# Cross-entropy over 32,000 classes: new row grouping, a third buffer, a tapered last group and transposed results

## The chip, the cores and the metric

The kernel runs on one core of one Trainium2 chip. The metric is the device time of one execution in microseconds (us).

## The reference

For each of 16 x 512 = 8192 rows of 32,000 float32 logits the loss is the log of the sum of exponentials minus the logit at the label. The kernels leave out the maximum, which this data (standard normal) allows.

```python
def reference(logits, labels):                  # (16, 512, 32000) f32, (16, 512) i32
    m = np.max(logits, axis=-1, keepdims=True)
    lse = np.log(np.sum(np.exp(logits - m), axis=-1)) + m.squeeze(-1)
    log_probs = logits - lse[..., np.newaxis]
    return -log_probs[np.arange(16)[:, None], np.arange(512), labels]
```

## The kernel before

The rows are cut into 64 groups of 128, one row per partition. Partition p holds rows 64p to 64p+63, so that one group takes rows 64 apart. SyncE (SP) issues the loads, ScalarE (ACT) takes the exponential in place and sums along the row, GpSimd (POOL) gathers the 8192 label logits with 64 indirect loads. HBM here names the memory of logits and results (`in_logits_dram` and `out_dram` in the profile); a transfer lands when the profile shows it complete. The first 61 groups are loaded in halves of 16,000 columns into two buffers, the last three in pieces of 4,000.

```python
lg_pg  = lg.rearrange("(p g) v -> p g v", g=G)              # group g: rows p*64 + g
out_pg = out.rearrange("b s -> (b s)").rearrange("(p g) -> p g", g=G)
data_pool = ctx.enter_context(tc.tile_pool(name="data", bufs=2))
fine_pool = ctx.enter_context(tc.tile_pool(name="fine", bufs=5))
nc.sync.dma_start(out=labs64[:], in_=labels_pg)             # before the logits
# ... indices, 64 gathers on GpSimd ...
for g in range(G):
    if g >= G - FINE_GROUPS:                                # 3 groups, WF = 4000
        # ... tf from fine_pool, 8 pieces a group, the same two calls ...
    else:
        for c in range(C):                                  # W = 16000, C = 2
            t = data_pool.tile([P, W], FP32)
            nc.sync.dma_start(out=t[:], in_=lg_pg[:, g, c * W:(c + 1) * W])
            nc.scalar.activation(out=t[:], in_=t[:], func=Exp, accum_out=stats_col(g, c))

def finalize(lo, hi):
    # ... totals = reduce_sum(stats), on VectorE ...
    # ... logsum = Ln(totals), on ScalarE ...
    # ... res = logsum - lab_logit, on VectorE ...
    nc.scalar.dma_start(out=out_pg[:, lo:hi], in_=res[:, lo:hi])
finalize(0, G - 1)
finalize(G - 1, G)        # 128 results, one per partition, 4 B each, 256 B apart in HBM
```

The softmax here doesn't subtract the row's maximum and nothing guards it: scores larger than these inputs give would overflow.

## Time and profile before

| | before |
|---|---|
| time, median of 3 | 2439.99 us |
| span of the profile | 2438.7 us |
| moved, mean rate | 1048.77 MB, 430 GB/s |
| start to start of two 16,000-column exponentials, steady part | 18.90 us |
| last load lands / last store issued / end | 2430.8 / 2436.21 / 2438.7 us |

The first lines are from the page of the kernel before. A row of digits shows the busy tenths of 40 slices of the span; GB/s is what the DMA engines moved in each.

```profile
span 2438.7 us, 851 instructions
...
ACT  4777766777677767777677767777677767777697
...
DMA  9999999999999999999999999999999999999998
GB/s 404 437 420 422 435 437 435 429 429 437 437 436 428 431 435 437 435 432 428 435 436 436 435 427 434 436 437 435 427 432 436 437 435 425 434 437 432 426 430 360
```

The DMA engines are full in every slice but the last (digit 9, 90% or more; a DMA share of 1.00 from 240 to 2380 us), ScalarE is not (72% of the span): the time to move 1048 MB is the time of the kernel. The chain of work that ended last, by line, on the same page:

```profile
DMA t<-in_logits_dram 61%; ACT t L85 34%; DMA tf<-in_logits_dram 2%; ACT tf L76 2%; ACT L101 0%; ACT L76 0%; ACTq L85 0%; ACT logsum L101 0%; SPq L84 0%; DVE res L105 0%; SPq L48 0%; ACTq L109 0%; ACTq L76 0%
```

The 34% of ScalarE does not mean that ScalarE limits anything. The chain goes from a load back to the exponential that freed its buffer. The costliest groups on that page tell it (busy us, mean ns of one | idle before it and what ended the idle time):

```profile
L85 ACT ACTIVATE t<-t 128x16000 f32<-128x16000 f32 x122 | 1651.4, 13536 | 642.9 <-DMA t<-in_logits_dram 642.9
...
L101 ACT ACT_TABLE_LOAD x2 | 2.6, 1283 | 0.0
```

Two exponentials of the steady part in the timeline, 18.90 us from start to start:

```profile
2297.67 13.54 ACT L85 ACTIVATE t<-t 128x16000 f32<-128x16000 f32 x1 [5.27 <-DMA t<-in_logits_dram]
...
2316.57 13.54 ACT L85 ACTIVATE t<-t 128x16000 f32<-128x16000 f32 x1 [5.27 <-DMA t<-in_logits_dram]
```

Each 13.5 us exponential waits 642.9 / 121 = 5.3 us for its load (the first of the 122 is booked apart).

A load lands 24.1 us after issue and the previous one lands 18.9 us before it, so 5.2 us of the 24.1 were spent in the queue: it never ran dry. The second line is the last store of all, 128 results of 4 B; it landed 1.4 us after issue. The timeline of the end (start us, us, engine, line):

```profile
2430.84 3.54 ACT L76 ACTIVATE tf<-tf 128x4000 f32<-128x4000 f32 x1 [1.11 <-DMA tf<-in_logits_dram]
...
2434.49 1.28 ACT L101 ACT_TABLE_LOAD   x1
...
2435.78 0.20 ACT L101 ACTIVATE logsum<-totals 128x1 f32<-128x1 f32 x1
2436.02 0.16 DVE L105 TENSOR_TENSOR res<-logsum,lab_logit 128x1 f32<-128x1 f32 x1 [1.35 <-ACT logsum L101]
2436.21 0.34 ACTq L109 DMA_DIRECT2D out_dram<-res  x1
```

The last exponential starts when the last load has landed. The store of the last group is issued at 2436.21 and the span ends at 2438.7, 2.5 us later.

### The profile page before, as it was taken

Reading aid. Unit: us, or ns where it says so; the run is one execution under the profiler, and the core shown is the slowest. Engines: PE = TensorE matmul, PEld = TensorE weight load, DVE = VectorE, ACT = ScalarE, POOL = GpSimd, SP = SyncE. Lnnn points to the kernel's source line nnn. Section 1 sums busy time; section 2 is a strip of 40 time slices with the busy share of each in tenths; the row PEclk is TensorE's granted clock in tenths of the full one; section 3 lists DMA queues with packets and bytes.
Section 4 is the critical chain, followed back from the end, with each engine's and each line's share of the span. In section 5 each row is a group of like instructions: output and inputs, shape, how many; then the busy total and the mean of one; then the engine's idle time right before and its main releaser. Section 6 shows DMA issues by size and latency. Waiting matters only on the chain.

```text
span 2438.7 us, 851 instructions
## 1 busy us (share of the span) xinstructions
DVE 1.7 (0%) x5; ACT 1754.4 (72%) x298; POOL 61.2 (3%) x70
## 2 busy tenths in 40 slices
DVE  0000000000000000000000000000000000000000
ACT  4777766777677767777677767777677767777697
POOL 3222000000000000000000000000000000000000
DMA  9999999999999999999999999999999999999998
GB/s 404 437 420 422 435 437 435 429 429 437 437 436 428 431 435 437 435 432 428 435 436 436 435 427 434 436 437 435 427 432 436 437 435 425 434 437 432 426 430 360
DMA packets 23510, 1048.77 MB, mean 430 GB/s; under 512 B 4688, under 2 KB 4816, under 8 KB 4816
## 3 DMA queue, kind: packets, MB, share of 16 engines
q1 hardware_dynamic: 21168, 1048.65, 99.6%
q0 software_dynamic: 2048, 0.04, 0.1%
q10 hardware_dynamic: 288, 0.03, 0.0%
q14 instruction: 6, 0.05, 0.0%
HBM read 1048.67 MB, written 0.03 MB: 430 GB/s over the span
## 4 chain that ended last, share of the span: by engine, by line
DMA 63%; ACT 36%; issue 0%; ACTq 0%; SPq 0%; DVE 0%
DMA t<-in_logits_dram 61%; ACT t L85 34%; DMA tf<-in_logits_dram 2%; ACT tf L76 2%; ACT L101 0%; ACT L76 0%; ACTq L85 0%; ACT logsum L101 0%; SPq L84 0%; DVE res L105 0%; SPq L48 0%; ACTq L109 0%; ACTq L76 0%
## 5 line engine op out<-in xcount | busy, mean ns | idle before, releaser
L85 ACT ACTIVATE t<-t 128x16000 f32<-128x16000 f32 x122 | 1651.4, 13536 | 642.9 <-DMA t<-in_logits_dram 642.9
L76 ACT ACTIVATE tf<-tf 128x4000 f32<-128x4000 f32 x24 | 84.7, 3530 | 14.6 <-DMA tf<-in_logits_dram 14.6
L57 POOL DMA_INDIRECT lab_logit<-in_logits_dram,idx x64 | 60.5, 945 | 186.8 <-DMA lab_logit<-in_logits_dram,idx 184.2
L85 ACT ACTIVATION_READ_ACCUMULATOR t<-t 128x1 f32 x122 | 22.7, 186 | 0.0
L85 ACT ACT_TABLE_LOAD x1 | 1.3, 1283 | 23.3 <-DMA t<-in_logits_dram 23.3
L76 ACT ACTIVATION_READ_ACCUMULATOR tf<-tf 128x1 f32 x24 | 4.5, 187 | 0.0
L101 ACT ACT_TABLE_LOAD x2 | 2.6, 1283 | 0.0
L96 DVE TENSOR_REDUCE totals<-stats 128x63 f32<-128x504 f32 x1 | 0.7, 678 | 2394.9 <-ACT tf L76 2394.9
L76 ACT ACT_TABLE_LOAD x1 | 1.3, 1283 | 0.8 <-DVE res L105 0.8
L66 DVE MEMSET stats<- 128x504 f32 x1 | 0.5, 478 | 0.9 <-PEq L127 0.9
L101 ACT ACTIVATE logsum<-totals 128x63 f32<-128x63 f32 (+1 forms) x2 | 0.5, 229 | 0.0
L105 DVE TENSOR_TENSOR res<-logsum,lab_logit 128x63 f32<-128x63 f32 (+1 forms) x2 | 0.4, 192 | 2.2 <-ACT logsum L101 2.2
L53 POOL TENSOR_TENSOR idx<-idx,labs 128x64 int32<-128x64 int32 x1 | 0.3, 318 | 1.8 <-DMA labs<-in_labels_dram 1.8
L96 DVE TENSOR_REDUCE totals<-stats_last 128x1 f32<-128x8 f32 x1 | 0.2, 161 | 36.4 <-ACT tf L76 36.4
L51 POOL IOTA idx<- 128x64 int32 x1 | 0.2, 172 | 0.4 <-PEq L138 0.4
L127 POOL MEMSET const-uint8-127<- 128x1 uint8 x1 | 0.1, 118 | 0.0
L127 POOL MEMSET const-bfloat16-1.0<- 128x1 bf16 x1 | 0.1, 113 | 0.0
L127 POOL MEMSET const-float32-0.0<- 128x1 f32 x1 | 0.1, 98 | 0.2 <-issue 0.2
L127 POOL MEMSET const-float32-1.0<- 128x1 f32 x1 | 0.1, 104 | 0.0
## 6 DMA issues: line engine op xcount, KB each, us to landing
t<-in_logits_dram SPq DMA_DIRECT2D x122, 8000.0 KB, 24.1
tf<-in_logits_dram SPq DMA_DIRECT2D x24, 2000.0 KB, 20.1
lab_logit<-in_logits_dram,idx POOLq DMA_INDIRECT x64, 33.4
labs<-in_labels_dram SPq DMA_DIRECT2D x1, 64.0 KB, 1.9
out_dram<-res ACTq DMA_DIRECT2D x1, 31.5 KB, 9.1
out_dram<-res ACTq DMA_DIRECT2D x1, 0.5 KB, 1.4
```

What stands on the lines that cost most here:

```text
L51: nc.gpsimd.iota(idx[:], pattern=[[V, G]], base=0, channel_multiplier=G * V)
L53: nc.gpsimd.tensor_tensor(out=idx[:], in0=idx[:], in1=labs32, op=mybir.AluOpType.add)
L57: nc.gpsimd.indirect_dma_start(out=lab_logit[:, g:g + 1], out_offset=None, in_=lg, in_offset=bass.IndirectOffsetOnAxis(ap=idx[:, g:g + 1], ...
L66: nc.vector.memset(stats[:], 0.0)
L76: nc.scalar.activation(out=tf[:], in_=tf[:], func=mybir.ActivationFunctionType.Exp, accum_out=stats_col(g, c),)
L85: nc.scalar.activation(out=t[:], in_=t[:], func=mybir.ActivationFunctionType.Exp, accum_out=stats_col(g, c),)
L96: nc.vector.reduce_sum(out=totals[:, lo:hi], in_=stats[:, lo:hi, :] if hi <= G - 1 else stats_last[:], axis=mybir.AxisListType.X,)
L101: nc.scalar.activation(out=logsum[:, lo:hi], in_=totals[:, lo:hi], func=mybir.ActivationFunctionType.Ln,)
L105: nc.vector.tensor_tensor(out=res[:, lo:hi], in0=logsum[:, lo:hi], in1=lab_logit[:, lo:hi], op=mybir.AluOpType.subtract,)
L127: nc = _bacc.Bacc("TRN2", target_bir_lowering=False, num_devices=1)
```

## The change

Its intent: hold more loads in flight (three buffers), end on pieces that shrink so that little work is left after the last load, load one table set that serves both exponential and log, and group neighbouring rows, which makes a group's results one contiguous run of the output. Labels and results then have to be transposed, on TensorE. The last group's 128 results are stored without a transpose. The core of the diff (cuts marked):

```diff
-    lg_pg = lg.rearrange("(p g) v -> p g v", g=G)
-    out_pg = out.rearrange("b s -> (b s)").rearrange("(p g) -> p g", g=G)
+    lg_gp = lg.rearrange("(g p) v -> g p v", p=P)
+    out_gp = out.rearrange("b s -> (b s)").rearrange("(g p) -> g p", p=P)
-    data_pool = ctx.enter_context(tc.tile_pool(name="data", bufs=2))
-    fine_pool = ctx.enter_context(tc.tile_pool(name="fine", bufs=5))
+    data = ctx.enter_context(tc.tile_pool(name="data", bufs=3))
+    TAPER = [11200, 8000, 5600, 3500, 2000, 1100, 600]
-    nc.sync.dma_start(out=labs64[:], in_=labels_pg)
+    nc.scalar.dma_start(out=labs64[:], in_=labels_gp)          # [64, 128]
+    nc.scalar.preload_act_table_set("natural_log_exp_and_others")
+    # ... labels to float, transposed on TensorE, back to int32 ...
-    # ... groups as above, the last 3 in pieces of 4000 ...
+    # ... 63 groups in halves of 16000 ...
+    spaces = [[0, 3, 5], [1, 2, 4], [6]]                       # pieces that share a buffer
+    for i, n in enumerate(TAPER):
+        nc.sync.dma_start(out=place[i], in_=lg_gp[G - 1, :, starts[i]:starts[i] + n])
+    for i, n in enumerate(TAPER):
+        nc.scalar.activation(out=place[i], in_=place[i], func=EXP, accum_out=sums_last[:, i:i + 1])
-    finalize(0, G - 1)
-    finalize(G - 1, G)
+    # ... totals, Ln, subtract for 63 groups ...
+    nc.tensor.transpose(res_t[:], res[:], ident[:])
+    nc.vector.tensor_copy(out=res_out[:], in_=res_t[:])
+    nc.scalar.dma_start(out=out_gp[0:G - 1, :], in_=res_out[:])
+    nc.vector.reduce_sum(out=part[:], in_=sums_last[:, 0:NT - 1], axis=mybir.AxisListType.X)
+    nc.scalar.activation(out=logsum_last[:], in_=sums_last[:, NT - 1:NT], func=LN, bias=part[:])
+    # ... subtract ...
+    nc.scalar.dma_start(out=out_gp[G - 1, :].unsqueeze(1), in_=res_last[:])
```

The scheduler puts the log and the store of the first 63 groups ahead of the seven tapered pieces in ScalarE's program.

More of the change, by code (lines that the diff above doesn't have):

```diff
@@ L7 @@
 from concourse._compat import with_exitstack
+from concourse.masks import make_identity
 FP32 = mybir.dt.float32
 I32 = mybir.dt.int32
+EXP = mybir.ActivationFunctionType.Exp
+LN = mybir.ActivationFunctionType.Ln
+ALU = mybir.AluOpType
 @with_exitstack
@@ L23 @@
     B, S, V = logits.shape
-    N = B * S
     P = 128
-    G = N // P
-    assert N % P == 0
+    G = B * S // P
     W = 16000
     C = V // W
-    assert V % W == 0
-    WF = 4000
-    CF = V // WF
-    FINE_GROUPS = 3
-    assert V % WF == 0
-    lg = logits.rearrange("b s v -> (b s) v")
-    lg_pg = lg.rearrange("(p g) v -> p g v", g=G)
-    labels_pg = labels.rearrange("b s -> (b s)").rearrange("(p g) -> p g", g=G)
-    out_pg = out.rearrange("b s -> (b s)").rearrange("(p g) -> p g", g=G)
@@ L43 @@
-    data_pool = ctx.enter_context(tc.tile_pool(name="data", bufs=2))
-    fine_pool = ctx.enter_context(tc.tile_pool(name="fine", bufs=5))
-    persist = ctx.enter_context(tc.tile_pool(name="persist", bufs=1))
-    labs64 = persist.tile([P, G], mybir.dt.int64)
-    nc.sync.dma_start(out=labs64[:], in_=labels_pg)
+    lg = logits.rearrange("b s v -> (b s) v")
+    lg_gp = lg.rearrange("(g p) v -> g p v", p=P)
+    labels_gp = labels.rearrange("b s -> (b s)").rearrange("(g p) -> g p", p=P)
+    out_gp = out.rearrange("b s -> (b s)").rearrange("(g p) -> g p", p=P)
@@ new lines @@
+    data = ctx.enter_context(tc.tile_pool(name="data", bufs=3))
+    persist = ctx.enter_context(tc.tile_pool(name="persist", bufs=1))
+    psum = ctx.enter_context(tc.tile_pool(name="psum", bufs=1, space=bass.MemoryType.PSUM))
+    TAPER = [11200, 8000, 5600, 3500, 2000, 1100, 600]
+    assert sum(TAPER) == V
+    NT = len(TAPER)
+    labs64 = persist.tile([G, P], mybir.dt.int64)
+    nc.scalar.dma_start(out=labs64[:], in_=labels_gp)
+    nc.scalar.preload_act_table_set("natural_log_exp_and_others")
@@ L50 @@
+    labs32 = labs64[:].bitcast(I32).rearrange("g (p two) -> g p two", two=2)[:, :, 0]
+    ident = persist.tile([P, P], FP32)
+    make_identity(nc, ident[:])
+    labs_f = persist.tile([G, P], FP32)
+    nc.vector.tensor_copy(out=labs_f[:], in_=labs32)
+    labs_t = psum.tile([P, G], FP32)
+    nc.tensor.transpose(labs_t[:], labs_f[:], ident[0:G, 0:G])
+    labs = persist.tile([P, G], I32)
+    nc.vector.tensor_copy(out=labs[:], in_=labs_t[:])
     idx = persist.tile([P, G], I32)
-    nc.gpsimd.iota(idx[:], pattern=[[V, G]], base=0, channel_multiplier=G * V)
@@ L52 @@
-    labs32 = labs64[:].bitcast(I32).rearrange("p (g two) -> p g two", two=2)[:, :, 0]
-    nc.gpsimd.tensor_tensor(out=idx[:], in0=idx[:], in1=labs32, op=mybir.AluOpType.add)
+    nc.gpsimd.iota(idx[:], pattern=[[P * (V >> 8), G]], base=0, channel_multiplier=V >> 8)
+    nc.vector.tensor_scalar(out=idx[:], in0=idx[:], scalar1=8, scalar2=None, op0=ALU.logical_shift_left)
+    nc.gpsimd.tensor_tensor(out=idx[:], in0=idx[:], in1=labs[:], op=ALU.add)
     lab_logit = persist.tile([P, G], FP32)
-    for g in range(G):
+    for g in [G - 1] + list(range(G - 1)):
@@ L62 @@
         )
-    stats = persist.tile([P, G - 1, CF], FP32)
-    stats_last = persist.tile([P, 1, CF], FP32)
-    nc.vector.memset(stats[:], 0.0)
-    def stats_col(g, c):
-        return stats[:, g, c:c + 1] if g < G - 1 else stats_last[:, 0, c:c + 1]
-    for g in range(G):
-        if g >= G - FINE_GROUPS:
-            for c in range(CF):
-                tf = fine_pool.tile([P, WF], FP32)
-                nc.sync.dma_start(out=tf[:], in_=lg_pg[:, g, c * WF:(c + 1) * WF])
-                nc.scalar.activation(
-                    out=tf[:], in_=tf[:],
-                    func=mybir.ActivationFunctionType.Exp,
-                    accum_out=stats_col(g, c),
-                )
-        else:
-            for c in range(C):
-                t = data_pool.tile([P, W], FP32)
-                nc.sync.dma_start(out=t[:], in_=lg_pg[:, g, c * W:(c + 1) * W])
-                nc.scalar.activation(
-                    out=t[:], in_=t[:],
-                    func=mybir.ActivationFunctionType.Exp,
-                    accum_out=stats_col(g, c),
-                )
@@ L91 @@
-    totals = persist.tile([P, G], FP32)
-    logsum = persist.tile([P, G], FP32)
-    res = persist.tile([P, G], FP32)
-    def finalize(lo, hi):
-        nc.vector.reduce_sum(
-            out=totals[:, lo:hi],
-            in_=stats[:, lo:hi, :] if hi <= G - 1 else stats_last[:],
-            axis=mybir.AxisListType.X,
-        )
-        nc.scalar.activation(
-            out=logsum[:, lo:hi], in_=totals[:, lo:hi],
-            func=mybir.ActivationFunctionType.Ln,
-        )
-        nc.vector.tensor_tensor(
-            out=res[:, lo:hi], in0=logsum[:, lo:hi], in1=lab_logit[:, lo:hi],
-            op=mybir.AluOpType.subtract,
-        )
-        nc.scalar.dma_start(out=out_pg[:, lo:hi], in_=res[:, lo:hi])
@@ L111 @@
-    finalize(0, G - 1)
-    finalize(G - 1, G)
+    sums = persist.tile([P, G, C], FP32)
+    for g in range(G - 1):
+        for c in range(C):
+            t = data.tile([P, W], FP32, tag="t")
+            nc.sync.dma_start(out=t[:], in_=lg_gp[g, :, c * W:(c + 1) * W])
+            nc.scalar.activation(out=t[:], in_=t[:], func=EXP, accum_out=sums[:, g, c:c + 1])
+    sums_last = persist.tile([P, NT], FP32)
+    spaces = [[0, 3, 5], [1, 2, 4], [6]]
+    starts = [sum(TAPER[:i]) for i in range(NT)]
@@ new lines @@
+    place = {}
+    for s in spaces:
+        t = data.tile([P, W], FP32, tag="t")
+        o = 0
+        for i in s:
+            place[i] = t[:, o:o + TAPER[i]]
+            o += TAPER[i]
+    for i, n in enumerate(TAPER):
+        nc.sync.dma_start(out=place[i], in_=lg_gp[G - 1, :, starts[i]:starts[i] + n])
+    for i, n in enumerate(TAPER):
+        nc.scalar.activation(out=place[i], in_=place[i], func=EXP, accum_out=sums_last[:, i:i + 1])
+    totals = persist.tile([P, G - 1], FP32)
+    logsum = persist.tile([P, G - 1], FP32)
@@ new lines @@
+    res = persist.tile([P, G - 1], FP32)
+    nc.vector.reduce_sum(out=totals[:], in_=sums[:, 0:G - 1, :], axis=mybir.AxisListType.X)
+    nc.scalar.activation(out=logsum[:], in_=totals[:], func=LN)
+    nc.vector.tensor_tensor(out=res[:], in0=logsum[:], in1=lab_logit[:, 0:G - 1], op=ALU.subtract)
+    res_t = psum.tile([G - 1, P], FP32)
+    nc.tensor.transpose(res_t[:], res[:], ident[:])
+    res_out = persist.tile([G - 1, P], FP32)
+    nc.vector.tensor_copy(out=res_out[:], in_=res_t[:])
+    nc.scalar.dma_start(out=out_gp[0:G - 1, :], in_=res_out[:])
@@ new lines @@
+    part = persist.tile([P, 1], FP32)
+    nc.vector.reduce_sum(out=part[:], in_=sums_last[:, 0:NT - 1], axis=mybir.AxisListType.X)
+    logsum_last = persist.tile([P, 1], FP32)
+    res_last = persist.tile([P, 1], FP32)
+    nc.scalar.activation(out=logsum_last[:], in_=sums_last[:, NT - 1:NT], func=LN, bias=part[:])
+    nc.vector.tensor_tensor(out=res_last[:], in0=logsum_last[:], in1=lab_logit[:, G - 1:G], op=ALU.subtract)
+    nc.scalar.dma_start(out=out_gp[G - 1, :].unsqueeze(1), in_=res_last[:])
```

## The prediction

> **What bounds it now.** The DMA engines. The slices of the span show them in the highest tenth in 39 of 40 slices, 430 GB/s on average; ScalarE (ACT) is 72% busy. In the timeline the 128x16000 exponentials start 18.90 us apart from about 250 us on, and each waits about 5.27 us for its load. 8.192 MB in 18.90 us is 433.4 GB/s. [...] the change moves the same 1048.6 MB. The chain of waits alternates 61% loads with 34% exponentials only because a buffer's exponential releases a load; that load then lands 24.07 us after issue, 5.2 us more than it takes to move, so the queue never runs dry.
>
> **What lies above pure streaming.** 128 x 18.90 = 2419 us; the span is 2438.7. The rest: start and first latency, about 3 us; the 64 label gathers of the first 240 us, which stretch the tile interval to 19.1 to 19.6 us, about 5 us in all; two stutters of 0.67 us; 24 fine loads at 4.76 us instead of 4.725, about 1 us; and 7.9 us after the last load lands (2430.8): exponential 3.54, table load 1.28, log 0.2, subtract 0.16, and 2.5 from store issue to end.
>
> **What the change does.**
> 1. Third buffer: the load queue is never empty with two, so about 0. ACT still waits 5.3 us per tile; issue to landing grows to about 43 us.
> 2. Row groups of 128 neighbouring rows instead of rows 64 apart (row pitch 128,000 B, was 8,192,000 B). [...]: 0. [...] no slowing shows in this trace.
> 3. Labels go through ACT's queue, two copies, a PE transpose: [...] same cost. Streaming starts about 0.4 us earlier.
> 4. Fine loads gone: -0.9 us; seven tapered loads cost about +0.2. Last load lands near 2429.7.
> 5. One table set [...]: four loads of 1.28 us become one; only the last lay on the end path: -1.28 us. The early one is hidden.
> 6. The taper. An ACT start-to-start costs 0.187 + 0.833 us per 1000 elements (3.52 at 4000). The seven pieces take 28.0 us of ACT; their loads 38. Tile 126 should land near 2391.7 and its exponential end near 2405.3. But in ACT's program order the log of the first 63 groups and their store issue now stand before the seven pieces, and that store also waits for a PE transpose and a PSUM copy: reduce 0.7, log and subtract 0.55, [...] issue 0.46: about 2.7 us. So the pieces run 2408 to 2436 with almost no wait, about 6 us behind the last landing, against 3.7 before. This returns what 4 and 5 gain. Then log, subtract, store: 3 us.
>
> Sum: span about 2439.2, measured time about 2440.5 (it lies 1.3 above the span): range 2437 to 2445. Faster by over 2%: 1%; within 2%: 97%; slower: 2%.
>
> **Right if:** interval 18.90 still; about 5 us gather loss; pieces of ACT back to back at the end; last landing about 6 us before the last exponential ends; one table load. **Wrong if:** the interval changes (HBM row pattern, deeper queue); gathers cost more or less; ACT waits for loads inside the taper (then the stall was cheap and it ends 2 to 3 us sooner).

The sum came to a span of about 2439.2 us and a time of about 2440.5 us, and one of its terms is the transpose and copy of point 6, an estimate that no trace supported. The 2.7 us of that point include it (the terms left, 0.7 + 0.55 + 0.46, make 1.71), and so do the 2408 to 2436 for the pieces. The 0 of point 2 stands on the trace of before alone (18.90 us, a DMA share of 1.00 from 240 to 2380 us). That one table set is enough in point 5 had not been shown by then; the page of the changed kernel shows it.

## More of the kernel before

Every run told here was in the fast state or, for two small kernels without timing rounds, of unknown state; the granted clock was 1.0 throughout. All comparisons of times are between fast runs. Runs that are compared with runs of the kernel before shared a chip with them; the three jobs of experiments ran on three different chips.

The lines of DMA issues give the size and the median us from issue to landing:

```profile
t<-in_logits_dram SPq DMA_DIRECT2D x122, 8000.0 KB, 24.1
...
out_dram<-res ACTq DMA_DIRECT2D x1, 0.5 KB, 1.4
```

## The result and the profile after

| | before | after |
|---|---|---|
| time, median (4 runs each, same rounds) | 2440.01 us | 2446.14 us |
| span of the profile | 2438.7 | 2444.1 |
| steady interval of exponentials | 18.90 | 18.90 |
| last exponential ends | 2434.47 | 2435.55 |
| last store issued | 2436.21 | 2436.09 |
| from there to the end | 2.5 | 8.0 |

The ratio is 1.0025 (95% interval 1.0011 to 1.0039), by the 2% rule the same. Ratios here are the mean time of one kernel's fast runs over that of the other's of the same rounds, so not quite the ratio of the medians quoted. The runs of before spread by 0.3 us and those of the changed kernel by 0.65 us, so 6.1 us is a real difference, and it lies outside the predicted range.

The page of the changed kernel:

```profile
span 2444.1 us, 792 instructions
...
DMA  9999999999999999999999999999999999999997
GB/s 420 419 434 421 426 429 435 436 436 436 434 430 427 435 436 436 436 434 432 428 433 436 436 435 436 433 430 429 435 436 436 435 434 432 428 434 435 435 436 304
```

The chain that ended last, by line, on the same page:

```profile
DMA t<-in_logits_dram 74%; ACT t L85 24%; ACT t L101 1%; ACTq L85 0%; ACTq L114 0%; PE res_t L111 0%; SPq L84 0%; ACT logsum_last L120 0%; DVE res_out L113 0%; DVE totals L107 0%; ACT logsum L108 0%; DVE res L109 0%; DVE res_last L121 0%; ACTq L101 0%
```

Only the last slice differs in kind, 304 GB/s instead of 360, because the span goes on for longer after the last load. The share of loads in the chain rose from 61% to 74%: with three buffers the chain goes through more queued loads and fewer exponentials; the stream itself is as fast. The costliest groups of the same page:

```profile
L85 ACT ACTIVATE t<-t 128x16000 f32<-128x16000 f32 x126 | 1705.7, 13537 | 685.0 <-DMA t<-in_logits_dram 685.0
...
L53 ACT ACT_TABLE_LOAD x1 | 1.3, 1283 | 1.3 <-PEq L137 1.3
```

The lines of DMA issues of the changed kernel (count, size, median us from issue to landing):

```profile
t<-in_logits_dram SPq DMA_DIRECT2D x126, 8000.0 KB, 43.0
...
out_dram<-res_last ACTq DMA_DIRECT2D x1, 0.5 KB, 7.1
```

The exponentials wait as before (685.0 / 126 = 5.4 us, the first wait included) and start 18.90 us apart as before:

```profile
2372.52 13.54 ACT L85 ACTIVATE t<-t 128x16000 f32<-128x16000 f32 x1 [5.27 <-DMA t<-in_logits_dram]
...
2391.42 13.54 ACT L85 ACTIVATE t<-t 128x16000 f32<-128x16000 f32 x1 [5.26 <-DMA t<-in_logits_dram]
```

Loads sit in the queue one tile longer, 43.0 us. One table load is left. The last line of the DMA issues is new: 512 B in 128 writes, as before, but 7.1 us from issue to landing instead of 1.4. The end in the timeline (`res_t` is the transpose of the first 63 groups' results):

```profile
2405.08 0.28 DVE L107 TENSOR_REDUCE totals<-sums 128x63 f32<-128x126 f32 x1 [2385.75 <-ACT t L85]
2405.40 0.26 ACT L108 ACTIVATE logsum<-totals 128x63 f32<-128x63 f32 x1 [0.35 <-DVE totals L107]
...
2406.48 0.28 DVE L113 COPY res_out<-res_t 63x128 f32<-63x128 f32 x1 [0.56 <-PE res_t L111]
...
2407.46 9.54 ACT L101 ACTIVATE t<-t 128x11200 f32<-128x11200 f32 x1 [1.80 <-DVE res_out L113]
...
2434.76 0.69 ACT L101 ACTIVATE t<-t 128x600 f32<-128x600 f32 x1
...
2435.57 0.30 ACT L120 ACTIVATE logsum_last<-sums_last,part 128x1 f32<-128x1 f32 x1
2435.90 0.16 DVE L121 TENSOR_TENSOR res_last<-logsum_last,lab_logit 128x1 f32<-128x1 f32 x1 [0.86 <-ACT logsum_last L120]
2436.09 0.37 ACTq L122 DMA_DIRECT2D out_dram<-res_last  x1
```

ScalarE stood from the last sum of the 63rd group (read by 2405.05) to 2407.46, less 0.26 us for the log, and then ran the seven pieces without a gap. The last store is issued 0.1 us earlier than before. The busy time by stretches (stretch, its length, each engine's busy time, clock, DMA share, GB/s) shows what followed:

```profile
core 0: us, PE busy (x) PEld busy (x) DVE busy (x) ACT busy (x) POOL busy (x), PEclk, DMA share, GB/s
...
2436.10:2438.00 1.90, 0.00 (x0) 0.00 (x0) 0.00 (x0) 0.00 (x0) 0.00 (x0) 1.00 0.04 0
2438.00:2444.10 6.10, 0.00 (x0) 0.00 (x0) 0.00 (x0) 0.00 (x0) 0.00 (x0) 1.00 0.00 0
```

The store's packets move within the first 1.9 us. After that no packet and no work of an engine is recorded; the store lands at about 2443.2 (2436.09 + 7.1), and the span ends at 2444.1. The packets themselves are no slower: in the trace of before the same stretch, 2.50 us long, has a DMA share of 0.03, so 2.50 x 0.03 and 1.90 x 0.04 are both about 0.08 us of busy time. The added time passes after the packets. So the whole loss of 5.4 us of span lies after the last instruction of compute, and the question is why a store of 512 B completes so late.

### The profile page after: what moved, and what is told of

The parts are those of the page before. It is cut to its first block, busy times and chain, and to the rows that moved or that the text cites. A ratio compares the mean times of both kernels' runs of the same rounds, so it can differ in the third digit from the quotient of the medians.

```text
span 2444.1 us, 792 instructions
## 1 busy us (share of the span) xinstructions
PE 0.8 (0%) x2; PEld 0.4 (0%) x2; DVE 1.7 (0%) x8; ACT 1747.4 (71%) x269; POOL 61.8 (3%) x72
## 4 chain that ended last, share of the span: by engine, by line
DMA 74%; ACT 25%; issue 0%; another core or an unknown queue 0%; ACTq 0%; DVE 0%; PE 0%; SPq 0%
DMA t<-in_logits_dram 74%; ACT t L85 24%; ACT t L101 1%; ACTq L85 0%; ACTq L114 0%; PE res_t L111 0%; SPq L84 0%; ACT logsum_last L120 0%; DVE res_out L113 0%; DVE totals L107 0%; ACT logsum L108 0%; DVE res L109 0%; DVE res_last L121 0%; ACTq L101 0%
## 5 line engine op out<-in xcount | busy, mean ns | idle before, releaser
L85 ACT ACTIVATE t<-t 128x16000 f32<-128x16000 f32 x126 | 1705.7, 13537 | 685.0 <-DMA t<-in_logits_dram 685.0
L101 ACT ACTIVATE t<-t 128x11200 f32<-128x11200 f32 (+6 forms) x7 | 28.0, 3999 | 1.8 <-DVE res_out L113 1.8
L59 DVE CAST labs_f<-labs 64x128 f32<-64x128 int32 x1 | 0.2, 218 | 18.4 <-DMA labs<-in_labels_dram 18.4
```

The costliest lines, as they stand in the source:

```text
L59: nc.vector.tensor_copy(out=labs_f[:], in_=labs32)
L85: nc.scalar.activation(out=t[:], in_=t[:], func=EXP, accum_out=sums[:, g, c:c + 1])
L101: nc.scalar.activation(out=place[i], in_=place[i], func=EXP, accum_out=sums_last[:, i:i + 1])
```

## The experiments

Theory A: 128 single-element writes that lie side by side hold back the store's completion. Theory B: the store of the first 63 groups is in its way. Theory C: mapping or taper slowed the rest. The first four runs shared a chip and a job with nine runs of before (2440.16 us).

### 1. The last store spread out

```diff
-    nc.scalar.dma_start(out=out_gp[G - 1, :].unsqueeze(1), in_=res_last[:])
+    out_pg = out.rearrange("b s -> (b s)").rearrange("(p g) -> p g", g=G)
+    nc.scalar.dma_start(out=out_pg[:, G - 1:G], in_=res_last[:])
```

> The changed kernel with one edit: the last store of 128 results writes its 4-byte elements 256 B apart, as the kernel before did, instead of side by side (wrong output on purpose, some of the first store is overwritten). Theory A (128 single-element writes that share a few lines of HBM hold back the store's completion): store issue to end falls from 8.0 us to about 2.5 us, the time from 2446.1 to about 2440.7 us. Theory B (the last store is late because the first store of 63 rows on the same queue, or its odd shape, is still in the way): no change, 2446 us. Theory C (the new row mapping or taper slowed the stream or ScalarE): no change in the end, 2446 us.

Measured: 2440.48 us, ratio to before 1.0002 (0.9988 to 1.0015). Its output is wrong, which doesn't matter for the time. Its line of DMA issues:

```profile
out_dram<-res_last ACTq DMA_DIRECT2D x1, 0.5 KB, 1.4
```

Landing is back at 1.4 us, from 7.1, with the same source, queue, size, number of writes and first store. Only the addresses differ. Theories B and C fall as causes of the loss.

### 2. The kernel before, its last store side by side

```diff
-        nc.scalar.dma_start(out=out_pg[:, lo:hi], in_=res[:, lo:hi])
+        if hi == G:
+            flat = out.rearrange("b s -> (b s)").rearrange("(g p) -> g p", p=P)
+            nc.scalar.dma_start(out=flat[G - 1, :].unsqueeze(1), in_=res[:, lo:hi])
+        else:
+            nc.scalar.dma_start(out=out_pg[:, lo:hi], in_=res[:, lo:hi])
```

> The kernel before with one edit: its last store writes the 128 results side by side, 4 B each (wrong output on purpose). Theory A: store issue to end grows from 2.5 us to about 8 us, the time from 2440.0 to about 2445.5 us. Theory B: no change, 2440.0 us, since the first store there has its old shape and landed long before.

Measured: 2445.92 us, ratio 1.0023 (1.0010 to 1.0037). Its output is wrong, which doesn't matter for the time. The line of its last store among the DMA issues of the end of its span:

```profile
out_dram<-res ACTq DMA_DIRECT2D x1, 0.5 KB, 7.1
```

The converse holds: this one line, put into the old kernel, costs what the whole change cost (2445.92 - 2440.16 = 5.8 us). Store issue to end is 8.2 us (2435.87 to 2444.1).

### 3. The last results as one row

```diff
-    nc.scalar.dma_start(out=out_gp[G - 1, :].unsqueeze(1), in_=res_last[:])
+    row_t = psum.tile([1, P], FP32)
+    nc.tensor.transpose(row_t[:], res_last[:], ident[:])
+    row = persist.tile([1, P], FP32)
+    nc.vector.tensor_copy(out=row[:], in_=row_t[:])
+    nc.scalar.dma_start(out=out_gp[G - 1:G, :], in_=row[:])
```

> The changed kernel, right output: the last 128 results are transposed into one partition by TensorE, copied out of PSUM and stored as one row of 512 B. The added transpose and copy cost about 0.8 us by the first store's pieces in the trace. Theory A: the store then ends about 2 us after issue, so the total falls by about 6.0 - 0.8 = 5.2 us less what the first-store chain says: about 2441.3 us. Theory B: about 2447 us, the same late store plus the transpose.

Measured: 2440.95 us, output right, ratio to before 1.0003 (0.9989 to 1.0017). Transpose and copy move the issue from 2436.09 to 2436.81, and the span then ends 2.0 us after the issue, at 2438.8 (the 2 expected was an estimate that no run had shown before). So 0.7 us of work buys 6.0 us:

```profile
2436.81 0.24 ACTq L126 DMA_DIRECT2D out_dram<-row  x1
```

The change without its one bad store is worth nothing against before: still 0.8 us slower at the median, which the interval does not tell from zero, though its five times all lie above the nine of before.

### 4. The first store on the other queue

```diff
-    nc.scalar.dma_start(out=out_gp[0:G - 1, :], in_=res_out[:])
+    nc.sync.dma_start(out=out_gp[0:G - 1, :], in_=res_out[:])
```

> The changed kernel with the store of the first 63 groups issued from the queue of SP instead of ScalarE's, so ScalarE no longer waits for the transpose and the copy before it takes up the last group (right output). The stall of 2.4 us between the 126th exponential and the first tapered one falls to about 0.7 us (reduce, then log), and as the tapered pieces run back to back the total falls by about 1.7 us, to about 2444.4 us, with the last store still 8.0 us long under theory A. Theory B (the two stores share a queue): the last store also becomes short, and the total falls by about 7 us, to 2439 us.

Measured: 2444.14 us, output right. The timeline of its end:

```profile
2406.33 0.26 ACT L108 ACTIVATE logsum<-totals 128x63 f32<-128x63 f32 x1 [0.35 <-DVE totals L107]
2406.49 9.52 ACT L101 ACTIVATE t<-t 128x11200 f32<-128x11200 f32 x1
...
2407.72 0.37 SPq L114 DMA_DIRECT2D out_dram<-res_out  x1
...
2435.10 0.35 ACTq L122 DMA_DIRECT2D out_dram<-res_last  x1
```

The log starts at 2406.33 and the first tapered piece at 2406.49; in the changed kernel 2.06 us lay between the two (2405.40 and 2407.46). ScalarE no longer waits for the transpose, the copy and the issue. The time fell by 2.0 us (2446.14, measured in another job, to 2444.14) against 1.7 expected. The last store stayed late (6.7 us to landing, 7.6 to the end), which is against theory B once more and confirms the predicted stall as a cost of its own.

### 5. The store by itself

Sixteen shapes of store in a chain, each waiting for the one before, three of each, no stream beside them; wrong output on purpose. The core:

```python
def view(n, w, s):                      # n rows of w elements, s elements apart
    return flat[0:n * s].rearrange("(p s) -> p s", s=s)[:, 0:w]
for _ in range(3):
    nc.scalar.dma_start(out=view(128, 1, 1), in_=src[0:128, 0:1])   # L42; then s = 2, 4, 8, 16, 32, 64
# ... fewer partitions; wider elements; one row of 512 B ...
```

> The store by itself, with no stream beside it: 16 shapes of store from ScalarE's queue, each three times, every one waiting for the one before (wrong output on purpose). Theory A1 (elements that share a small unit of HBM hold each other back, so it is the number of writes per unit that counts): 128 writes of 4 B at a spacing of 4 B land 7 us after issue, and as the spacing doubles the time falls in steps to about 1.4 us at 256 B, with half the excess gone at each doubling; 16 adjacent writes of 4 B land in under 2.5 us; 128 adjacent writes of 64 B in about 1.5 us. Theory A2 (the whole 512 B region is one serial resource and what counts is the number of writes to it, not the spacing): about 7 us up to a spacing where the region spans more than one unit, then a sudden fall. Theory D (it is the 128 separate descriptors): all spacings alike, which the run with the spread store already speaks against. One row of 512 B: about 1.4 us.

The timeline for spacings of 4, 8, 16, 32 and 64 B (L42, L44, L46, L48, L50); the second column runs from the start of the first issue to the end of the third issue, not to the landing:

```profile
2.95 17.15 ACTq L42 DMA_DIRECT2D out_dram<-src  x3
29.44 8.52 ACTq L44 DMA_DIRECT2D out_dram<-src  x3
41.31 4.25 ACTq L46 DMA_DIRECT2D out_dram<-src  x3
47.36 3.20 ACTq L48 DMA_DIRECT2D out_dram<-src  x3
51.69 3.21 ACTq L50 DMA_DIRECT2D out_dram<-src  x3
```

One store takes a third of the step from one line's start to the next: (29.44 - 2.95) / 3 = 8.8 us at 4 B, 4.0 at 8 B, 2.0 at 16 B, 1.4 at 32 B. The profile's median from issue to landing agrees: 9.2, 4.1, 2.1, 1.4, and 1.4 for 64, 128 and 256 B. (Three stores of each shape are few: the three at 4 B took 7.6 to 9.7, where 7 had been expected.) The size of the element matters little: 128 writes of 8 B side by side took 3.4 to landing, of 16 B 1.8, of 32 and 64 B 1.4, of 256 B 1.5. Theory D (the number of descriptors) falls. The fall is gradual, so the sudden step of theory A2 is not there; but it is steeper than the halving that A1 expected: above 1.4 us there are 7.8, 2.7 and 0.7 us at 4, 8 and 16 B. A1 also missed the 16 adjacent writes: 3.0 us measured, under 2.5 expected. One row of 512 B took about 1.1 us. A1's own premise, that the writes per small unit count, does not hold alone either: 16, 32, 64 and 128 adjacent writes put the same 8 writes into every 32 B, and yet took 3.0, 5.5, 7.6 and 8.8 us by the same thirds.

### 6. Who holds whom back

The same chain with other shapes. Its output is wrong, which doesn't matter for the time. L42, L44, L46 and L48: 2, 4, 8 and 16 partitions with one element each, side by side. L50 and L52: 16 partitions at 8 and 32 B. L54: 128 side by side. L56, L58, L60, L62: 128 partitions 256 B apart, with 8 elements each at 32, 16, 8 and 4 B. L64: 128 single elements 256 B apart.

> The store by itself again, to tell who holds whom back (wrong output on purpose; each store waits for the one before, three of each). First 2, 4, 8, 16 partitions with one 4-byte element each, side by side; then 16 at spacings of 8 and 32 B; 128 side by side as the control (9.2 us in the last run); then 128 partitions 256 B apart with 8 elements each, the elements 32, 16, 8 and 4 B apart; then 128 single elements 256 B apart as the floor (1.4 us). Theory E (only writes of different partitions that fall into one small unit hold each other back): side by side, the time grows by about 0.1 us with each further partition, 1.4, 1.6, 2.0, 3.0 us, the 16 at 32 B spacing take 1.4 us, and the 8 elements of one partition take the same time at 32, 16, 8 and 4 B. Theory F (any two small writes to one unit do, whoever writes): the time of the 8 elements of one partition rises as they move together, by several us from 32 B to 8 B (at 4 B they may go out as one write of 32 B, then the floor).

The timeline, from L46 on:

```profile
9.72 2.61 ACTq L46 DMA_DIRECT2D out_dram<-src  x3
13.22 3.83 ACTq L48 DMA_DIRECT2D out_dram<-src  x3
19.18 5.50 ACTq L50 DMA_DIRECT2D out_dram<-src  x3
26.66 2.98 ACTq L52 DMA_DIRECT2D out_dram<-src  x3
30.65 15.78 ACTq L54 DMA_DIRECT2D out_dram<-src  x3
54.41 9.85 ACTq L56 DMA_DIRECT2D out_dram<-src  x3
...
83.20 10.43 ACTq L60 DMA_DIRECT2D out_dram<-src  x3
98.46 3.22 ACTq L62 DMA_DIRECT2D out_dram<-src  x3
```

By the same thirds (the starts not shown are 2.98 for L42, 6.24 for L44 and 102.78 for L64): 1.09, 1.16, 1.17 and 1.99 us for 2, 4, 8 and 16 partitions; 2.49 for 16 at 8 B and 1.33 at 32 B; 7.92 for 128 side by side; 4.68, 4.91, 5.09 and 1.44 for the 8 elements of one partition. Theory F, several us between 32 B and 8 B, is not what happened: 4.68 against 5.09. Theory E holds in that part, but its growth by 0.1 us with each partition fell: nothing up to 8 partitions, then a rise, and the 16 took 1.99 here but 2.97 in run 5, on another chip. The stores of 8 elements that lie apart (32, 16 and 8 B) have 1024 writes each; the number of writes may set their time and could hide short holds, which was not tested. At 4 B the 8 elements went out as one write: the queue of the stores shows 11,028 packets in all, and the shapes alone would need 13,242 with 1024 writes there too, and 10,554 with 128. What it is in HBM or in the DMA engines that makes such writes wait is not settled by these runs; what is shown is where it begins in these shapes: 16 partitions took 1.99 us at 4 B and 2.49 at 8 B, against 1.33 at 32 B, and 128 took 2.0 at 16 B, against 1.4 at 32 B (run 5), while 8 side by side took 1.17, no longer than 4 (1.16).

### 7. Both repairs

```diff
 # as in 3, and
-    nc.scalar.dma_start(out=out_gp[0:G - 1, :], in_=res_out[:])
+    nc.sync.dma_start(out=out_gp[0:G - 1, :], in_=res_out[:])
```

> Both repairs at once, right output: the last 128 results stored as one row, and the first store issued from SP's queue. If the two savings simply add (row store 2440.95 in the last job against 2446.14; SP queue a stall of 2.5 us cut to 0.6 us): 2440.95 - 1.9 = 2439.0 us, 0.05% below the kernel before. If ScalarE no longer ends the taper (its pieces wait for loads) less than 1 us is saved: 2440 us.

Measured: 2438.97 us, output right, beside nine runs of before at 2440.20; ratio 0.9995 (0.9982 to 1.0009). The savings add. The interval includes 1, though the five times all lie below the nine of before.

### 8. A longer taper

```diff
-    TAPER = [11200, 8000, 5600, 3500, 2000, 1100, 600]
+    PREV = [13000, 11000, 8000]                                             # group 62
+    TAPER = [7000, 6000, 5000, 4000, 3200, 2400, 1800, 1300, 800, 500]      # group 63
+    spaces = [[0], [1], [2, 3], [4, 5, 6], [7, 8, 9, 10, 11, 12]]
 # ... the main loop ends one group earlier; the rest as in 7 ...
```

> The former, with the taper spread over the last two row groups (13000, 11000, 8000, then 7000 down to 500 in ten pieces), right output. Theory: the last exponentials lag the last landing because ScalarE takes 28.0 us for the seven pieces from a late start; with gentler steps and the pause for the log in the middle it should end about 1.5 us after the last landing instead of 4.4 us: 2439.0 - 2.9 + about 0.2 for six more loads = 2436.3 us. Rival: small loads cost more of the stream than 0.04 us each, and the gain is lost: 2438 us or more.

Measured: 2436.65 us, output right, same rounds as 7; ratio 0.9986 (0.9972 to 0.9999). Groups are counted from 0 in the cut, so group 63 is the last. From its timeline, the first piece of the last group, the last piece and the last store:

```profile
2400.02 6.04 ACT L109 ACTIVATE t<-t 128x7000 f32<-128x7000 f32 x1 [0.79 <-DMA t<-in_logits_dram]
...
2430.64 0.60 ACT L109 ACTIVATE t<-t 128x500 f32<-128x500 f32 x1
...
2432.63 0.48 ACTq L134 DMA_DIRECT2D out_dram<-row  x1
```

After the log ScalarE waits for a load again (0.79 us), so the pause for the log has become free. The last sum is read at 2431.34, against 2433.89 in run 7, and the last load landed at about 2429.95 (issued at 2407.15, 22.8 us to landing): a lag of 1.4 us, near the 1.5 expected. In run 7 the last load landed at 2429.76 (2405.36 + 24.4), so the six more small loads cost about the 0.2 us assumed. This is the fastest version, 3.55 us below before; by the 2% rule it is still the same.

### 9. Two buffers instead of three

```diff
-    data = ctx.enter_context(tc.tile_pool(name="data", bufs=3))
+    data = ctx.enter_context(tc.tile_pool(name="data", bufs=2))
-    spaces = [[0, 3, 5], [1, 2, 4], [6]]
+    spaces = [[0, 3, 5], [1, 2, 4, 6]]
 # tiles are W + 200 wide so that the second space holds 16200 columns
```

> The changed kernel with two buffers of 16200 instead of three of 16000. Theory (the third buffer gives the stream nothing, since the queue never ran dry with two): the exponentials stay 18.90 us apart, issue to landing falls from 43.0 back to about 24.1 us, and the time is 2446.1 us, or up to 0.6 us more because the tapered loads of the second buffer are issued only after the 126th exponential. Rival (the third buffer has a value that something else in the change hides): intervals above 18.90 us or a time above 2448 us.

Measured: 2446.84 us, output right, in the rounds of runs 7 and 8. The intervals are 18.90 us, issue to landing is 24.1 us, and one tapered piece waits 0.16 us for its load. The changed kernel itself was not run again in these rounds; across two jobs the difference is 0.7 us, of which before shows 0.2 (2440.20 against 2440.01); up to 0.6 had been expected. The third buffer gives the stream nothing.

## Why the prediction was wrong

The step that failed is the last sentence of point 6, "Then log, subtract, store: 3 us." It took the 2.5 us from store issue to end out of the old trace, where the 128 elements lie 256 B apart, and carried them over to a store with the same shape and size whose elements lie 4 B apart. From the last exponential to the end it took 8.6 us (2435.55 to 2444.1), of which the store took 8.0. Runs 1 and 2 show that the spacing alone makes the difference, in both directions.

The sum, against the profile: the predicted span of 2439.2 had the last store issued at about 2436.7 (2439.2 less 2.5); it was issued at 2436.09, which gives -0.6. The store adds 8.0 - 2.5 = +5.5. Together 4.9, the difference of 2444.1 and 2439.2. A second, smaller term was off: time minus span was taken as 1.3 us from the median time of before and a page whose run was not named. Where runs list both, it is 1.8 us (2440.22 and 2438.4 for before, 2445.91 and 2444.1 for after). The two terms make 4.9 + 0.5 = 5.4 of the 5.64 us between 2440.5 and 2446.14; the rest is that the profiled run was 0.23 us faster than the median.

Point by point:

- The bound was right: interval 18.90 us in both kernels, and in both 433.4 GB/s (8.192 MB in 18.90 us); in both the DMA share is 1.00 from 240 to 2380 us.
- Third buffer about 0, landing about 43 us: right (43.0; run 9).
- Row mapping 0 for the loads: right (18.90 us in both). For the last store the new mapping was the cause of the loss: the prediction priced the new grouping on the way in and not on the way out.
- Labels: the gathers start at 20.0 us instead of 3.6, 16 us later; how much later the forecast put them was an estimate without a trace, and was far too low. The labels landed at 18.4 us; they were issued at 0.75 us, at the same moment as the first load (0.74) and not ahead of it. In the trace of before they were issued at 0.74, the first load at 1.18, and the labels landed in 1.9 us. That this is why was not tested. It costs nothing: the gathers' stretch of the intervals is again about 5 us (the 15 intervals from 23.10 to 311.47 take 4.9 us more than 15 x 18.90).
- Fine loads gone, tapered loads in: last landing predicted near 2429.7. The 600-column load was issued at 2405.07 and landed 24.5 us later, at 2429.6. Right.
- One table load instead of four: right, 1.28 us off the end (from the last sum to the log 1.31 us before, 2434.47 to 2435.78, and 0.02 after, 2435.55 to 2435.57).
- Taper and ScalarE stall: right and shown apart. The pieces ran 2407.46 to 2435.55 back to back (2408 to 2436 predicted), ending 6.0 us behind the last landing. The stall before them was 2.4 us (2405.05 to 2407.46) against 2.7; its transpose and copy took 0.82 (2405.97 to 2406.79). Run 4 takes the stall away and gains 2.0 us; runs 7 and 8, with the row store, end 1.2 and 3.55 us below before.

So all that the change set out to gain, the fine loads and the table load, was given back by the taper's late start, as predicted, and the store came on top.

## What to carry to other kernels

Price the stores by the addresses that they write, not by their bytes: one element from each of many partitions, side by side in HBM, completed 5.5 us later in the kernel than the same elements 256 B apart (8.0 against 2.5 from issue to end), and by itself 7.8 us later than 32 B apart (9.2 against 1.4), and at the end of the changed kernel nothing hid it (5.4 us more span), nor at the end of the kernel before with the same store (run 2, 5.8 us more time). Transposing such a column into one row cost 0.7 us here. When a term of a sum is copied from an old trace, ask first whether everything that the term depends on, the address pattern too, is the same in the new kernel.
